# A planned order for the small work behind an expert's twelve weight blocks, in a hybrid GLA / pooling / mixture-of-experts layer

## The chip, the cores and the metric

The kernel runs on one core of one Trainium2 chip. The metric is the device time of one execution in microseconds (us); the time of a kernel is the median of its runs. The engines are PE (TensorE: matrix products and transposes), DVE (VectorE), ACT (ScalarE), POOL (GpSimd) and SP (SyncE, which here only issues DMAs).

## The reference

One layer: a mixer (gated linear attention beside multi-scale pooling), then 32 experts of which each token uses 4, then a final norm. The change touches only the expert part and the norm behind it. Cut to these:

```python
def moe(h, w_router, b_router, w_gu, b_gu, w_down, b_down):     # h: 1024 tokens x 1024
    logits = xt @ w_router + b_router                           # 32 experts
    top_vals, top_idx = lax.top_k(logits, 4)
    weights = jax.nn.softmax(top_vals, axis=-1)
    # tokens sorted by expert, each expert padded to blocks of 128
    def expert_block(xblk, e):
        gate, up = jnp.split(xblk @ w_gu[e] + b_gu[e], 2, axis=-1)     # 1024 -> 2 x 1024
        gate = jnp.minimum(gate, 7.0)
        up = jnp.clip(up, -7.0, 7.0)
        act = (up + 1.0) * gate * jax.nn.sigmoid(1.702 * gate)
        return act @ w_down[e] + b_down[e]                             # 1024 -> 1024
    # each token sums its 4 experts' rows, weighted
h = h + g2 * moe(modulate(rmsnorm(h, norm_mlp_w), sh2, sc2), ...)
return rmsnorm(h, final_norm_w)
```

All of it is float32. The kernel gets near float32 products out of TensorE by splitting each operand into a high and a low part and adding three products.

## The kernel before

The first quarter of the time is the mixer, which the change leaves alone. Then come 32 passes, one for each expert, in an order made of "heavy" experts (H, ranks 0 to 15 by number of tokens, which have more tokens than one block of 128 rows and so one or two remainder groups of 32 slots) and "light" ones (L, no remainder): HHHLLH, then LH twelve times, then LL.

**Blocks.** An expert's weights come as twelve blocks of 1 MB: eight of `w_gu` (128 rows x 2048) and four of `w_down`. SP loads them in program order into eight slots (`ring`, `mix`, `ringx`), five blocks ahead (`load_to`). Two blocks ahead, `split_to` makes the high and low parts in a tile `hl`, of which there are three: ACT copies (L131), then DVE subtracts (L132). PE then multiplies: `gu_chunk(e, k)` does 12 matmuls of 512 columns into `pG` for each of the eight k, `dn_chunk(e, k0)` 12 into `pD` for each of four k0. After k = 3 and k = 7 a heavy expert's `gu_chunk` also does its remainder products into `pR`, from the raw slots. A pass of the outer loop `e` runs the eight gate/up blocks of expert e and then the four down blocks of expert e - 1, so a block's place in the pass is 0 to 11.

**Small work between the blocks.** PE is kept in program order (`T.strict`), so what is called after a block stands in PE's queue there. DVE, ACT and POOL instructions are placed by the scheduler, unless pinned (`keep_in_program_order`). The pieces are:

- `prep_a(e-1, 0)`, `(…, 1)`: four transposes of the last expert's activation (`at`) into the one PSUM bank `pps`, an ACT copy and a DVE subtract into `aT`; `prep_a(e-1, 2)`: two transposes (`ppr`) of a remainder, an ACT copy, for a heavy e - 1 only.
- `prep_x(e+1, 0)`, `(…, 1)`, `(…, 2)`: the same for the next expert's gathered tokens (`xg` into `xT`, `xq` into `xqT`); part 2 for a heavy e + 1 only.
- `prep_sel(e+2)`, `prep_route(e+2)`: slot selection on DVE, 8 to 72 small matmuls (`pq`), gathers of expert e + 2's rows on POOL.
- `act(e)`: gate and up clipped and multiplied, three DVE instructions and one on ACT (L1533 to L1536).

`pps`, `ppr`, `pq`, and at the start `pbq`, `px`, `pyw`, `pcs`, `pblk`, all take the pool `ptr` with the tag `t`, which has one buffer: a piece's PE instruction waits until the piece before it has been read out of that bank.

The places are fixed by

```python
    A_AT, X_AT = (0, 2, 3), (4, 6, 7)
```

with `prep_sel` at 6 and `prep_route` at 9 (for e = 0 at 7). Ahead of the first pass stand, in PE's order, the four bias products `bias_rows`, `route_weights`, and the slot weights of experts 0 and 1; between the passes 0 and 1 stands `route_blocks`.

**The end.** `final_out` adds for each of eight token tiles the last expert's share (L1658, DVE), squares and sums it (ACT), takes the root (two POOL instructions of one column, L1662 and L1663), and scales by it and the norm's weight: in one DVE instruction (L1671), but for the tiles 0 and 2 on ACT (L1668) and POOL (L1669). Then the tile is stored.

Of the kernel before, what the change touches and what calls it, by code (L numbers as in the profile page):

```python
# [9 lines left out]
F32 = mybir.dt.float32  # L10
# [4 lines left out]
AF = mybir.ActivationFunctionType  # L15
ALU = mybir.AluOpType
# [3 lines left out]
P = 128  # L20
D = 1024
# [5 lines left out]
NE = 32  # L27
# [25 lines left out]
def tile_hybrid_layer(ctx: ExitStack, tc: tile.TileContext, x, c, ctx_in, c_ctx, w_ada, b_ada, norm_mix_w,  # L53
# [1173 lines left out]
    def route_weights():  # L1227
# [19 lines left out]
        for j in range(4):  # L1247
            S.activation(g2r[32 * j:32 * j + 32], g2b[32 * j:32 * j + 32, 256 * j:256 * j + 256], AF.Copy)

    def route_blocks():  # L1250

        erb = tp.tile([NE, 2 * NE + 1], F32, name="erb")
        V.tensor_copy(erb[:, 0:NE], pe_[:NE, 0:NE])
        nb = tp.tile([NE, 1], F32, name="nb")
        tmp1 = tp.tile([NE, 1], F32, name="tmp1")
        over = tp.tile([NE, 1], F32, name="over")
        pcs = ptr.tile([NE, 8], F32, name="pcs", tag="t")
        T.matmul(pcs[:, 0:1], eqr[:NE], cnt[:NE], start=True, stop=True)
        V.tensor_tensor(over, pcs[:, 0:1], cap4, op=ALU.subtract)
        for j in range(7):  # L1260
            dst = nb if j == 0 else tmp1
            V.tensor_scalar(dst, over, float(P * j), None, op0=ALU.is_gt)
            if j:
                V.tensor_tensor(nb, nb, tmp1, op=ALU.add)
        pb = ptr.tile([P, 3, NE], F32, name="pblk", tag="t")
        nbb = tp.tile([NE, 2, MAXBLK], F32, name="nbb")
        V.tensor_copy(nbb[:, 0], nb.to_broadcast([NE, MAXBLK]))
        V.tensor_copy(nbb[:, 1], capc.to_broadcast([NE, MAXBLK]))
        T.matmul(pb[:MAXBLK, 0], nbb[:, 0], linc, start=True, stop=True)
        T.matmul(pb[:MAXBLK, 1], nbb[:, 0], ident[:NE, :NE], start=True, stop=True)  # L1270
# [40 lines left out]

    bq = ap.tile([P, 4, 512], BF16, name="bq", tag="bq")

    def bias_rows():
        perm = ap.tile([P, 2 * D], BF16, name="perm", tag="y")[:, 0:1536].rearrange(
            "p (a q n j i) -> p a q n j i", a=3, q=4, n=4, j=8)
        V.memset(perm, 0.0)
        for i in range(3):
            V.tensor_copy(perm[:, i, :, :, :, i], pbd.rearrange("p n (q j) -> p q n j", q=4))
        for q in range(4):  # L1320
            pb = ptr.tile([P, 512], F32, name="pbq", tag="t")
            for i in range(3):
                T.matmul(pb, perm[:, i, q].rearrange("p n j i -> p (n j i)"), bt[:, i], start=(i == 0), stop=(i == 2))
            S.activation(bq[:, q], pb, AF.Copy)
# [108 lines left out]
    def prep_a(e, part):  # L1433
        if part == 0:
            R["aT", e] = (xp.tile([P, 2, KT, P], F32R, name="aTl", tag="xT") if e == NE - 1 else
                          ap.tile([P, 2, KT, P], F32R, name="aT", tag="aT"))
        if part < 2:
            transpose_split(R["act", e], part, R["aT", e])
        else:
            R["aqT", e] = []  # L1440
            for src in R["actq", e]:
                dst = ap.tile([P, 2, P], F32, name="aqT", tag="aqT", bufs=2)
                transpose_rem(src, dst)
                R["aqT", e].append(dst)
# [82 lines left out]
                                 rquart[:, 2 * h + j // 2, jj:jj + 1].to_broadcast([P, CAPR]),  # L1527
                                 bq[:, s_, 256 * (j % 2):256 * (j % 2) + 256], start=False, stop=False)

    def act_unit(gate, up, w, tag, bufs):  # L1530
        g = ap.tile([P, w], F32, name="ag", tag="ag" + tag)
        t = ap.tile([P, w], F32, name="at", tag="at" + tag, bufs=bufs)
        V.tensor_scalar(g, gate, 7.0, None, op0=ALU.min)  # L1533
        S.activation(g, g, AF.Gelu_apprx_sigmoid)  # L1534
        V.tensor_scalar(t, up, 1.0, -6.0, op0=ALU.add, op1=ALU.max)
        V.scalar_tensor_tensor(t, t, 8.0, g, op0=ALU.min, op1=ALU.mult)  # L1536
        return t

    def act(e):
        g, rs = GU.pop(e)  # L1540
        R["actq", e] = [act_unit(r[:, 0:256], r[:, 256:512], 256, "r", 2) for r in rs]
        R["act", e] = act_unit(g[:, 0:2].rearrange("p a n -> p (a n)"), g[:, 2:4].rearrange("p a n -> p (a n)"),
                               D, "m", 1)

    def dn_start(e):
        d = (pgu.tile([P, 4, 512], F32, name="pDl", tag="g")[:, 2:4] if e == NE - 1 else
# [148 lines left out]
    with tc.high_priority():  # L1695
# [18 lines left out]
        pinned[0] = False  # L1714
        for p_ in range(3):
            prep_x(0, p_)
    bias_rows()
    route_weights()
    dump("posm", posm)
    dump("wfull", lg)  # L1720
    for i in range(2):
        pq = ptr.tile([P, 3, 8], F32, name="pq", tag="t")
        route_main(i, pq, slice(2, 5))
        route_rem(i, pq, slice(2, 5))
        slot_weights(i, pq)
    T.strict = True
    A_AT, X_AT = (0, 2, 3), (4, 6, 7)
    for e in range(nexp + 1):
        if e < nexp:
            gu_start(e)  # L1730
            for k in range(KT):
                advance()
                gu_chunk(e, k)

                if e > 0 and k in A_AT:
                    prep_a(e - 1, A_AT.index(k))
                if e + 1 < NE and k in X_AT:
                    prep_x(e + 1, X_AT.index(k))
                if e + 2 < NE and k == 6:
                    prep_sel(e + 2)  # L1740
                if e + 2 < NE and k == 7 and e == 0:
                    prep_route(e + 2)
        if e > 0:
            dn_start(e - 1)
            for k0 in range(0, KT, 2):
                advance()
                with tc.high_priority() if e == NE - 1 else ExitStack():
                    if k0 == 0 and e < nexp:
                        act(e)
                    if e == NE - 1 and k0 >= 4:  # L1750
                        prep_a(e, k0 // 2 - 2)
                dn_chunk(e - 1, k0)
                if k0 == 2 and e + 2 < NE:
                    prep_route(e + 2)
# [158 lines left out]
```

## Time and profile before

| | |
|---|---|
| median of 3 runs | 2020.53 us (2020.08 to 2022.52) |
| profiled execution: its time, and its span | 2023.95 us, 2022.2 us |
| PE busy, share of the span | 1872.5 us, 93% |
| DVE busy | 1544.6 us, 76% |
| ACT busy | 1139.1 us, 56% |
| POOL busy | 339.0 us, 17% |
| mean of TensorE's granted clock | 0.971 of full speed |
| two passes (one H, one L) in the steady part | 88.2 us |

The profiled execution is one execution; its time is 3.4 us above the median. The span is what the profile's clock shows from the first instruction to the last, and 1.75 us lie around it. Busy shares are averages over the whole program: the expert passes, from 558 us on, have a PE that is almost never idle, and the stretch from 508 to 558 us has one that mostly is.

### The profile page before, as it was taken

To read this page: it belongs to the slowest core of one execution; us is meant where nothing else is said; L and a number is where in the kernel's file an instruction comes from. 1 tells how busy PE (TensorE), PEld (TensorE's weight loads), DVE (VectorE), ACT (ScalarE), POOL (GpSimd) and SP (SyncE) were. 2 spreads that over 40 slices of the span, in tenths; PEclk is the share of its full clock that TensorE was granted. 3 is DMA by queue.
4 is the path that set the end of the run, shared out by engine and by line. 5 is a ranking of instruction groups with operands and counts; after the bars stand their busy time and mean duration, and the time that the engine had idled before them with its cause. 6 is when DMAs were issued, how large, how long until landed. Compare 5 with 4: busy or idle time off the path is not lost.

```text
span 2022.2 us, 29473 instructions
## 1 busy us (share of the span) xinstructions
PE 1872.5 (93%) x11472; PEld 1373.6 (68%) x11473; DVE 1544.6 (76%) x1606; ACT 1139.1 (56%) x1267; POOL 339.0 (17%) x238
## 2 busy tenths in 40 slices
PE   7999998999389999999999999999999999999995
PEld 4776776787256677767677676767667676767774
DVE  5486478658667788878788788878878887887887
ACT  4564456644435566656566565656656565665664
POOL 2010043011300221111111111111111111111114
PEclk9999998999599999999999999999999999999998
DMA  9285422243635789968888796888879688887985
GB/s 343 78 295 180 152 75 92 77 151 134 237 159 199 285 327 332 357 248 355 297 317 326 283 367 246 348 305 316 324 286 366 246 343 302 322 324 290 365 305 178
DMA packets 125528, 532.33 MB, mean 263 GB/s; under 512 B 13196, under 2 KB 27328, under 8 KB 90568
## 3 DMA queue, kind: packets, MB, share of 16 engines
q1 hardware_dynamic: 109464, 481.82, 61.2%
q0 software_dynamic: 15344, 48.01, 9.1%
q8 instruction: 92, 1.51, 0.3%
q10 hardware_dynamic: 576, 0.56, 0.1%
q14 instruction: 52, 0.43, 0.1%
HBM read 497.68 MB, written 32.67 MB: 262 GB/s over the span
## 4 chain that ended last, share of the span: by engine, by line
PE 78%; DVE 9%; ACT 5%; issue 4%; DMA 3%; POOL 1%; SPq 0%; POOLq 0%; DVEq 0%; ACTq 0%
PE pG L74 31%; PE pD L74 17%; PE pa L74 12%; PE pR L74 9%; ACT hl L131 4%; DVE hl L132 3%; PE pw L74 2%; PE pps L79 2%; PE pt L74 2%; DMA ringx<-in_w_down_dram 1%; PE pt L79 1%; PE ppr L79 1%; PE pDl L74 1%; PE pq L74 1%; DVE xT L1413 1%
## 5 line engine op out<-in xcount | busy, mean ns | idle before, releaser
L74 PE MATMUL pG<-hl,xT 128*128 128x512 f32 x3072 | 769.2, 402 | 0.0
L74 PEld LDWEIGHTS pG<-hl,xT 128*128 128x128 f32 x3072 | 566.0, 189 | 144.3 <-issue 21.9
L132 DVE TENSOR_TENSOR hl<-ring,hl 128x2048 fp32r<-128x2048 f32 (+2 forms) x199 | 398.4, 2009 | 168.9 <-ACT hl L131 167.4
L131 ACT ACTIVATE hl<-ring 128x2048 fp32r<-128x2048 f32 (+2 forms) x199 | 331.9, 1670 | 304.2 <-PE pG L74 168.2
L132 DVE TENSOR_TENSOR hl<-mix,hl 128x2048 fp32r<-128x2048 f32 x144 | 329.5, 2290 | 121.8 <-ACT hl L131 121.8
L131 ACT ACTIVATE hl<-mix 128x2048 fp32r<-128x2048 f32 (+1 forms) x146 | 277.7, 1902 | 234.4 <-PE pG L74 168.7
L74 PE MATMUL pD<-hl,aT 128*128 128x512 f32 x1488 | 365.5, 401 | 0.3 <-DVE hl L132 0.3
L74 PEld LDWEIGHTS pD<-hl,aT 128*128 128x128 f32 x1488 | 276.6, 189 | 76.0 <-issue 11.7
L132 DVE TENSOR_TENSOR hl<-ringx,hl 128x2048 fp32r<-128x2048 f32 x96 | 219.7, 2288 | 24.5 <-ACT hl L131 24.2
L131 ACT ACTIVATE hl<-ringx 128x2048 fp32r<-128x2048 f32 x96 | 184.0, 1917 | 93.0 <-PE pG L74 54.5
L1374 POOL DMA_INDIRECT xg<-h2d,ix x32 | 64.4, 2012 | 884.3 <-DVE ix L1370 424.8
L74 PE MATMUL pa<-hl,hi 128*128 128x512 f32 x544 | 180.4, 417 | 5.7 <-DVE wsg L760 3.7
L1588 POOL DMA_INDIRECT acc<-y,ix x31 | 104.5, 3369 | 156.8 <-DVE y L1583 156.8
L74 PEld LDWEIGHTS pa<-hl,hi 128*128 128x128 f32 x544 | 102.5, 197 | 31.4 <-DVE wsg L760 4.8
L74 PE MATMUL pa<-hl,lo 128*128 128x512 f32 x272 | 107.7, 407 | 0.0
L74 PE MATMUL pa<-hi,hl 128*128 128x512 f32 (+1 forms) x288 | 95.6, 395 | 1.0 <-ACT hi L400 1.0
L74 PEld LDWEIGHTS pa<-hi,hl 128*128 128x128 f32 x288 | 54.9, 193 | 16.2 <-ACT hi L400 2.9
L1593 POOL DMA_INDIRECT acc<-yq,ixr x17 | 34.0, 1999 | 163.5 <-DMA acc<-y,ix 150.1
L74 PEld LDWEIGHTS pa<-hl,lo 128*128 128x128 f32 x272 | 52.8, 196 | 11.9 <-issue 1.1
L74 PE MATMUL pa<-lo,hl 128*128 128x512 f32 (+1 forms) x144 | 55.3, 387 | 1.8 <-DVE lo L401 1.8
L74 PE MATMUL pR<-ring,xqT 128*32 128x512 f32 x408 | 53.3, 596 | 0.0
L1534 ACT ACTIVATE ag<-ag 128x1024 f32<-128x1024 f32 (+1 forms) x49 | 40.7, 831 | 20.7 <-DVE ag L1533 20.7
(392 smaller groups left out, 2031.2 us busy)
## 6 DMA issues: line engine op xcount, KB each, us to landing
ring<-in_w_gu_dram SPq DMA_DIRECT2D x96, 1024.0 KB, 15.3
mix<-in_w_gu_dram SPq DMA_DIRECT2D x96, 1024.0 KB
ringx<-in_w_gu_dram SPq DMA_DIRECT2D x64, 1024.0 KB, 6.8
ring<-in_w_down_dram SPq DMA_DIRECT2D x48, 1024.0 KB
mix<-in_w_down_dram SPq DMA_DIRECT2D x48, 1024.0 KB, 18.6
ringx<-in_w_down_dram SPq DMA_DIRECT2D x32, 1024.0 KB, 16.5
ring<-in_w_in_dram SPq DMA_DIRECT2D x32, 512.0 KB, 5.4
ring<-in_w_ada_dram SPq DMA_DIRECT2D x16, 1024.0 KB, 5.8
```

The source lines that it names most:

```text
L74: i = nc.tensor.matmul(*a, **k)
L79: i = nc.tensor.transpose(*a, **k)
L131: S.activation(hl[:, 0], src, AF.Copy)
L132: i = eng.tensor_tensor(hl[:, 1], src, hl[:, 0].bitcast(F32), op=ALU.subtract)
L1374: nc.gpsimd.indirect_dma_start(out=xg, out_offset=None, in_=h2d, in_offset=bass.IndirectOffsetOnAxis(ap=ix[:, 0:1], axis=0))
L1413: V.tensor_tensor(dst[:, 1, part], pp, dst[:, 0, part].bitcast(F32), op=ALU.subtract)
L1534: S.activation(g, g, AF.Gelu_apprx_sigmoid)
L1588: nc.gpsimd.indirect_dma_start(out=acc, out_offset=bass.IndirectOffsetOnAxis(ap=ix[:, 0:1], axis=0), in_=y, in_offset=None, compute_op=ALU ...
L1593: nc.gpsimd.indirect_dma_start(out=acc4, out_offset=bass.IndirectOffsetOnAxis(ap=ixr[g][:, 0:1], axis=0), in_=yq, in_offset=None, compute_ ...
```

## The change

The places of the pieces become a table, `plan(e)`, which holds for each of the twelve places of a pass the functions to call behind that block.

- `prep_a` goes from places (0, 2, 3) to (0, 2, 4), `prep_x` from (4, 6, 7) to (5, 7, 9), `prep_sel` from 6 to 8, `prep_route` from 9 to 10.
- The four bias products, `route_weights` and the slot weights of experts 0 and 1, which stood ahead of expert 0's first block, go behind blocks of passes 0 and 1. `route_blocks` is cut in three; its counting and its row building go behind blocks 3 and 6 of pass 1. Expert 2's `prep_route` goes from place 7 of pass 0 to place 1 of pass 1.
- For the last expert `act` is called ahead of `advance()` (which issues the next load and split) and its four instructions are pinned.
- The final norm's scaling is done on DVE for all eight tiles.

```diff
-    bias_rows()
-    route_weights()
-    for i in range(2):
+    perm = bias_perm()
+
+    def weigh(i):
         pq = ptr.tile([P, 3, 8], F32, name="pq", tag="t")
         route_main(i, pq, slice(2, 5))
         route_rem(i, pq, slice(2, 5))
         slot_weights(i, pq)
...
+    def plan(e):
+        todo = {}
+
+        def at(k, f, *a):
+            todo.setdefault(k, []).append((f, a))
+        if e == 0:
+            for k, q in ((0, 0), (2, 2), (4, 1)):
+                at(k, bias_rows, perm, q)
+            at(1, route_weights)
+            at(3, prep_x, 1, 2)
+            at(5, weigh, 0)
+            at(5, weigh, 1)
+            at(6, prep_x, 1, 0)
+            at(7, prep_x, 1, 1)
+            at(7, prep_sel, 2)
+            return todo
...
+        for k, p in ((0, 0), (2, 1), (4, 2)):
+            at(k, prep_a, e - 1, p)
+        if e + 1 < NE:
+            for k, p in ((5, 0), (7, 1), (9, 2)):
+                at(k, prep_x, e + 1, p)
+        if e == 1:
+            at(1, prep_route, 2)
+            at(3, route_counts)
+            at(6, route_rows)
+            at(11, bias_rows, perm, 3)
+        if e + 2 < NE:
+            at(8, prep_sel, e + 2)
+            at(10, prep_route, e + 2)
+        return todo
...
-                if e > 0 and k in A_AT:
-                    prep_a(e - 1, A_AT.index(k))
-                if e + 1 < NE and k in X_AT:
-                    prep_x(e + 1, X_AT.index(k))
...
+                if k0 == 0 and e == NE - 1:
+                    act(e)
                 advance()
+                if k0 == 0 and e < NE - 1:
+                    act(e)
...
-        FP = dbg.get('FP', (0, 2))
+        FP = dbg.get('FP', ())
```

**What stands where.** Three places show how the instructions moved. First PE at the start of the expert passes; `pps` and `ppr` are the transposes of expert 0's tokens, `pG<-hl,xT` a gate/up block, `pbq` the bias products, `px` and `pyw` those of `route_weights`. Before:

```order
L79 MATMUL pps<-ident,xg_4733 128x128 x8
L79 MATMUL ppr<-ident,xq 128x128 x4
L74 LDWEIGHTS perm
L74 MATMUL pbq<-mix,perm 128x512
...
L79 MATMUL px<-ident,lg 128x128 x2
L74 MATMUL pyw<-pbd,wT 128x128 x2
L74 LDWEIGHTS sel
L74 MATMUL pq<-info,sel 128x3
```

And of the change:

```order
L79 MATMUL pps<-ident,xg_4733 128x128 x8
L79 MATMUL ppr<-ident,xq 128x128 x4
L74 MATMUL pG<-hl,xT 128x512 x12
...
L74 MATMUL pG<-hl,xT 128x512 x12
L79 MATMUL px<-ident,lg 128x128 x2
L74 MATMUL pyw<-pbd,wT 128x128 x2
L74 MATMUL pG<-hl,xT 128x512 x12
```

The first block of expert 0 now stands right behind its transposes, and the products for biases and weights stand between blocks.

Second, PE in a light expert's pass between two heavy ones, from the second `prep_a` transposes on. Before:

```order
L79 MATMUL pps<-ident,at 128x128 x4
L74 MATMUL pG<-hl,xT 128x512 x12
L79 MATMUL ppr<-ident,at 128x128 x2
L74 MATMUL pG<-hl,xT 128x512 x12
L79 MATMUL pps<-ident,xg_7762 128x128 x4
L74 MATMUL pG<-hl,xT 128x512 x24
L79 MATMUL pps<-ident,xg_7762 128x128 x4
L74 MATMUL pG<-hl,xT 128x512 x12
L79 MATMUL ppr<-ident,xq 128x128 x2
L74 MATMUL pD<-hl,aT 128x512 x24
```

And of the change:

```order
L79 MATMUL pps<-ident,at 128x128 x4
L74 MATMUL pG<-hl,xT 128x512 x24
L79 MATMUL ppr<-ident,at 128x128 x2
L74 MATMUL pG<-hl,xT 128x512 x12
L79 MATMUL pps<-ident,xg_7778 128x128 x4
L74 MATMUL pG<-hl,xT 128x512 x24
L79 MATMUL pps<-ident,xg_7778 128x128 x4
L74 MATMUL pD<-hl,aT 128x512 x24
L79 MATMUL ppr<-ident,xq 128x128 x2
L74 MATMUL pD<-hl,aT 128x512 x12
```

Between a `pps` and the `ppr` behind it there are now two blocks (x24) where there was one (x12); the second `pps` of the next expert's tokens stands behind the last gate/up block.

Third, DVE at the same place, from the first subtract for `xT` on (`ag`, `at` are `act`). Before:

```order
L1413 TENSOR_TENSOR xT<-pps,xT 128x512
L132 TENSOR_TENSOR hl<-mix,hl 128x2048
L132 TENSOR_TENSOR hl<-ringx_4706,hl 128x2048
L1413 TENSOR_TENSOR xT<-pps,xT 128x512
L1533 TENSOR_SCALAR ag<-pG 128x1024
L1535 TENSOR_SCALAR at<-pG 128x1024
L132 TENSOR_TENSOR hl<-ringx_4707,hl 128x2048
L1536 SCALAR_TENSOR_TENSOR at<-at,ag 128x1024
```

And of the change:

```order
L1423 TENSOR_TENSOR xT<-pps,xT 128x512
L132 TENSOR_TENSOR hl<-ringx_4706,hl 128x2048
L1543 TENSOR_SCALAR ag<-pG 128x1024
L1545 TENSOR_SCALAR at<-pG 128x1024
L132 TENSOR_TENSOR hl<-ringx_4707,hl 128x2048
L1423 TENSOR_TENSOR xT<-pps,xT 128x512
L1546 SCALAR_TENSOR_TENSOR at<-at,ag 128x1024
```

The second subtract for `xT` now stands behind the first two instructions of `act` and one more split. For the last expert, DVE's and ACT's rows from `act` to the last store of the down products are the same in both kernels, in the same order, up to the final norm.

## Rows read from the trace of the kernel before

**Rows 1.** The chain that ended last, by engine, shares of the span.
```profile
PE 78%; DVE 9%; ACT 5%; issue 4%; DMA 3%; POOL 1%; SPq 0%; POOLq 0%; DVEq 0%; ACTq 0%
```

**Rows 2.** Waits of the whole span: us in total, times, longest us.
```profile
PE ppr L79 <- DVE xT L1413: 24.0, 14, 2.1
PE ppr L79 <- DVE aT L1413: 23.8, 14, 1.7
```

**Rows 3.** Timeline, a light pass: start us, us, what, [idle before <-releaser].
```profile
1025.50 0.44 PE L79 MATMUL ppr<-ident,at 128*128 128x128 f32 x2 [1.70 <-DVE aT L1413]
...
1034.61 0.60 PE L79 MATMUL pps<-ident,xg 128*128 128x128 f32 x4
...
1039.71 0.44 PE L79 MATMUL ppr<-ident,xq 128*128 128x128 f32 x2 [1.70 <-DVE xT L1413]
1039.90 5.84 PE L74 MATMUL pD<-hl,aT 128*128 128x512 f32 x24
...
1036.76 2.29 DVE L132 TENSOR_TENSOR hl<-ringx,hl 128x2048 fp32r<-128x2048 f32 x1 [0.50 <-ACT hl L131]
1038.97 0.68 DVE L1413 TENSOR_TENSOR xT<-pps,xT 128x512 fp32r<-128x512 f32 x1
1039.57 1.22 DVE L1533 TENSOR_SCALAR ag<-pG 128x1024 f32<-128x1024 f32 x1
1040.70 1.22 DVE L1535 TENSOR_SCALAR at<-pG 128x1024 f32<-128x1024 f32 x1
...
1034.81 1.92 ACT L131 ACTIVATE hl<-ringx 128x2048 fp32r<-128x2048 f32 x1 [0.88 <-PE pG L74]
```

**Rows 4.** Stretches: us, busy of PE, PEld, DVE, ACT, POOL, PEclk, DMA, GB/s.
```profile
540.00:558.00 18.00, 8.73 (x130) 4.15 (x129) 5.23 (x7) 7.69 (x9) 0.00 (x0) 0.50 0.68 280
558.00:566.00 8.00, 8.00 (x31) 6.37 (x26) 2.69 (x4) 1.92 (x1) 0.00 (x0) 0.70 0.01 2
...
970.00:1058.00 88.00, 84.59 (x516) 61.70 (x515) 72.56 (x51) 53.07 (x37) 14.66 (x6) 1.00 0.83 314
```

**Rows 5.** Timeline of PE, passes 0 and 1 and what stands ahead.
```profile
538.55 0.69 PE L79 MATMUL ppr<-ident,xq 128*128 128x128 f32 x2 [1.39 <-ACT xqT L1419]
...
556.11 0.94 PE L74 MATMUL pq<-info,sel 128*128 128x3 bf16 x72 [5.36 <-ACT info L1246]
...
557.96 13.62 PE L74 MATMUL pG<-hl,xT 128*128 128x512 f32 x48
...
598.54 0.44 PE L79 MATMUL ppr<-ident,xq 128*128 128x128 f32 x2
...
605.02 0.31 PE L74 MATMUL pblk<-linc,nbb 32*32 32x32 f32 x2 [3.64 <-DVE nbb L1267]
...
610.66 0.60 PE L79 MATMUL pps<-ident,at 128*128 128x128 f32 x4
```

**Rows 6.** Timeline, the final norm.
```profile
1992.97 2.36 DVE L1658 TENSOR_TENSOR ring<-pF,ring 128x1024 f32<-128x1024 f32 x2 [0.90 <-PE pF L74]
...
1997.69 2.42 POOL L1669 TENSOR_TENSOR ring<-ring,fw 128x1024 f32<-128x1024 f32 x1 [0.15 <-ACT ring L1668]
...
1997.96 3.23 DVE L1671 SCALAR_TENSOR_TENSOR ring<-ring,fr,fw 128x1024 f32<-128x1024 f32 x1
...
2003.38 1.27 DVE L1671 SCALAR_TENSOR_TENSOR ring<-ring,fr,fw 128x1024 f32<-128x1024 f32 x1
...
2011.62 1.32 POOL L1662 TENSOR_SCALAR fs<-fs 128x1 f32<-128x1 f32 x1
...
2013.62 1.28 DVE L1671 SCALAR_TENSOR_TENSOR mix<-mix,fr,fw 128x1024 f32<-128x1024 f32 x1 [0.77 <-POOL fr L1663]
```

**Rows 7.** Timeline, PE in the last pass.
```profile
1968.95 1.02 PE L79 MATMUL pps<-ident,at 128*128 128x128 f32 x4 [3.84 <-DVE at L1536]
```

**Rows 8.** Transfers into `ringx`, 960 to 1062 us: ns, first and last start, landing.
```profile
L1467 SPq DMA_DIRECT2D ringx<-in_w_down_dram x2: 373/378/384, 1013.0 to 1016.4; - x2
...
DMA to landing us min/median/max: 6.5/7.4/16.4
```

More of the change, by code (lines that the diff above doesn't have):

```diff
@@ L1248, in route_weights, with route_counts @@
             S.activation(g2r[32 * j:32 * j + 32], g2b[32 * j:32 * j + 32, 256 * j:256 * j + 256], AF.Copy)
+    B = {}
     def route_blocks():
-        erb = tp.tile([NE, 2 * NE + 1], F32, name="erb")
+        erb = B["erb"] = tp.tile([NE, 2 * NE + 1], F32, name="erb")
         V.tensor_copy(erb[:, 0:NE], pe_[:NE, 0:NE])
+    def route_counts():
         nb = tp.tile([NE, 1], F32, name="nb")
@@ L1264, in route_blocks, with route_rows @@
                 V.tensor_tensor(nb, nb, tmp1, op=ALU.add)
-        pb = ptr.tile([P, 3, NE], F32, name="pblk", tag="t")
-        nbb = tp.tile([NE, 2, MAXBLK], F32, name="nbb")
+        nbb = B["nbb"] = tp.tile([NE, 2, MAXBLK], F32, name="nbb")
         V.tensor_copy(nbb[:, 0], nb.to_broadcast([NE, MAXBLK]))
         V.tensor_copy(nbb[:, 1], capc.to_broadcast([NE, MAXBLK]))
+    def route_rows():
+        nbb, erb = B["nbb"], B["erb"]
+        pb = ptr.tile([P, 3, NE], F32, name="pblk", tag="t")
         T.matmul(pb[:MAXBLK, 0], nbb[:, 0], linc, start=True, stop=True)
@@ L1312, in tile_hybrid_layer, with bias_perm @@
     bq = ap.tile([P, 4, 512], BF16, name="bq", tag="bq")
-    def bias_rows():
+    def bias_perm():
         perm = ap.tile([P, 2 * D], BF16, name="perm", tag="y")[:, 0:1536].rearrange(
@@ L1319, in bias_rows @@
             V.tensor_copy(perm[:, i, :, :, :, i], pbd.rearrange("p n (q j) -> p q n j", q=4))
[L1320 to L1324, printed above, removed]
+        return perm
+    def bias_rows(perm, q):
+        pb = ptr.tile([P, 512], F32, name="pbq", tag="t")
+        for i in range(3):
+            T.matmul(pb, perm[:, i, q].rearrange("p n j i -> p (n j i)"), bt[:, i], start=(i == 0), stop=(i == 2))
+        S.activation(bq[:, q], pb, AF.Copy)
     slots = RS + [MS[0], MS[2], MS[3]] + RX
@@ L1528, in gu_chunk, with act_unit @@
                                  bq[:, s_, 256 * (j % 2):256 * (j % 2) + 256], start=False, stop=False)
-    def act_unit(gate, up, w, tag, bufs):
+    def act_unit(gate, up, w, tag, bufs, pin=lambda i: i):
         g = ap.tile([P, w], F32, name="ag", tag="ag" + tag)
         t = ap.tile([P, w], F32, name="at", tag="at" + tag, bufs=bufs)
[L1533 to L1536, printed above, removed]
+        pin(V.tensor_scalar(g, gate, 7.0, None, op0=ALU.min))
+        pin(S.activation(g, g, AF.Gelu_apprx_sigmoid))
+        pin(V.tensor_scalar(t, up, 1.0, -6.0, op0=ALU.add, op1=ALU.max))
+        pin(V.scalar_tensor_tensor(t, t, 8.0, g, op0=ALU.min, op1=ALU.mult))
         return t
@@ L1542, in act @@
         R["act", e] = act_unit(g[:, 0:2].rearrange("p a n -> p (a n)"), g[:, 2:4].rearrange("p a n -> p (a n)"),
-                               D, "m", 1)
+                               D, "m", 1, *([tc.keep_in_program_order] if e == NE - 1 else []))
     def dn_start(e):
@@ L1716, in tile_hybrid_layer @@
             prep_x(0, p_)
-    bias_rows()
-    route_weights()
-    dump("posm", posm)
-    dump("wfull", lg)
-    for i in range(2):
+    perm = bias_perm()
+    def weigh(i):
         pq = ptr.tile([P, 3, 8], F32, name="pq", tag="t")
@@ L1725, in tile_hybrid_layer, with extras @@
         slot_weights(i, pq)
+    def plan(e):
[13 more added lines that the diff above has]
+            return todo
+        if e == NE:
+            return todo
[12 more added lines that the diff above has]
+            at(10, prep_route, e + 2)
+        return todo
     T.strict = True
-    A_AT, X_AT = (0, 2, 3), (4, 6, 7)
     for e in range(nexp + 1):
+        todo = plan(e)
+        def extras(k):
+            for f, a in todo.pop(k, ()):
+                f(*a)
         if e < nexp:
@@ L1733, in tile_hybrid_layer @@
                 gu_chunk(e, k)
-                if e > 0 and k in A_AT:
-                    prep_a(e - 1, A_AT.index(k))
-                if e + 1 < NE and k in X_AT:
-                    prep_x(e + 1, X_AT.index(k))
[L1739 to L1742, printed above, removed]
+                extras(k)
         if e > 0:
@@ L1745, in tile_hybrid_layer @@
             for k0 in range(0, KT, 2):
+                if k0 == 0 and e == NE - 1:
+                    act(e)
                 advance()
+                if k0 == 0 and e < NE - 1:
+                    act(e)
                 with tc.high_priority() if e == NE - 1 else ExitStack():
-                    if k0 == 0 and e < nexp:
-                        act(e)
                     if e == NE - 1 and k0 >= 4:
@@ L1752, in tile_hybrid_layer @@
                 dn_chunk(e - 1, k0)
-                if k0 == 2 and e + 2 < NE:
-                    prep_route(e + 2)
+                if e < nexp:
+                    extras(KT + k0 // 2)
                 if e == NE:
```

## The prediction

> **What bounds the kernel now.** I read the chain of work that ended last first: PE carries 78% of it, DVE 9% [rows 1]. So the question for each part of the profile is when PE stands still, and for what. The list of waits, for PE alone, answers it for the expert passes: a `ppr` transpose waits 14 times for a DVE subtract into `xT` and 14 times for one into `aT`, 47.8 us together [rows 2], and no other wait of PE recurs there. The timeline of a light pass shows why: `ppr` stands one block behind `pps`, both need the one bank of `ptr`, and the bank is free only when DVE has subtracted, which it does behind a split of 2.29 us. That is 1.70 us each time, twice in a light pass between heavy ones [rows 3]. The stretch table then says what else could bind: in 88 us of steady passes PE is busy 84.59 us at the full clock, DVE 72.56, ACT 53.07, and the transfers' share is 0.83 [rows 4]. PE is the bound, the rest has 12% or more to spare.
>
> Two stretches differ. [...] And between passes 0 and 1 PE waits for the block counting, 3.64 us in its longest wait [rows 5]. At the end, the norm is a chain of DVE instructions [rows 6].
>
> **The change part by part.**
>
> *The first two passes.* Expert 0's last `ppr` ends at 538.55 + 0.69 = 539.24; its first block starts at 557.96 [rows 5]. In the change it starts at 539.24: its weights and transposes are ready, since the splits ran ahead. From there I rebuild pass 0. Before it took 557.96 to 598.54 = 40.6 us, with both `xT` transposes and the slow start of the clock (mean 0.70 from 558 to 566 [rows 4]), which I keep. The moved work is what PE did from 540 to 558, 8.73 us at half clock, so 4.4 at full clock; 0.4 of it, the fourth bias, goes to pass 1: 4.0. New waits: `route_weights` sends `px` to ACT and wants it back between two blocks; on ACT a split copy of 1.92 us (as in [rows 3]) stands ahead: 2.0. The two weight steps share the bank with each other and with the transposes behind them, one DVE reduce each, partly behind a split: 1.0. Sum 47.6, so pass 0 ends at 586.8, and the first block of expert 1 (2.9 us, half of the 5.84 us of two blocks in [rows 3]) at 589.7. Before, that block ended at 610.66, where `pps` follows it [rows 5]. Gain 20.9. Pass 1 then pays: routing of expert 2, counting, the last bias, 1.7 of PE work at full clock; `pblk` one block behind `pps`, the same wait as today's 1.70 [rows 3]; and some 35 small DVE instructions, 1.0 of lateness. Together 4.4. Net 16.5 us. If the waits were nil and PE took the clock up sooner, 20; if each new step waited for a whole split on ACT and on DVE (1.92 + 2.29, twice more), 8.
>
> *The `prep_a` waits.* Two blocks now lie between `pps` and `ppr`. The bank is free 5.0 us after `pps` ends as I read the timeline (the waiting `ppr` starts 1.70 late behind one block of 2.9 and its overlap), and two blocks take 5.7 to 5.8. All 14 vanish: 23.8 us [rows 2]. The bounds are 0 and 23.8; the margin of 0.7 is on each of 14 equal passes, so I take the whole.
>
> *The `prep_x` waits.* Here something takes their place. The second `pps` now stands behind the last gate/up block, and its subtract on DVE behind `act`, as the order shows. Let 0 be that block's end. Before, the split for the second down block began on ACT 0.2 us after the block before had ended (1034.61 to 1034.81), on DVE 1.95 later, and held DVE 2.21 [rows 3]. With that block's end at -2.9, DVE is free at -2.9 + 0.2 + 1.95 + 2.21 = 1.46. Then come the two clips, 1.13 each from start to start (3.72), a split 2.21 (5.93), the subtract 0.68 (6.61), and `ppr` 0.06 later. PE does the transposes in 0.35 and two down blocks in 5.8: it is there at 6.15. So `ppr` waits about 0.6 in place of 1.70. One of the 14 belongs to expert 0's own transposes ahead of the passes and stays; 13 go from 1.70 to 0.6: 14.3 us. The bounds: 0 if the wait stays whole, 22 if it goes. The next in line, the split for the last down block, is ready on DVE at about 9.9, where PE wants it at about 10: no spare, no wait. Behind it `prep_route` stands a block later and gives that block's time back.
>
> In a heavy pass the remainder products (3.6 us) stand between, and the same walk leaves every split about 1 us early.
>
> *The last expert's `act`.* The rows on DVE and ACT are the same in the same order, so nothing is gained: the wait of 3.84 us there stays [rows 7]. 0.
>
> *The final norm.* Eight adds at 1.18 (2.36 for two) and eight scalings, each 1.27 but 1.19 from start to start: 9.4 + 9.5 us on DVE, plus the last wait for the root, 0.77, and 0.2 for a row to arrive: 20.0 from 1992.97 on. Before, the last scaling ended at 2014.90, after 21.9 [rows 6]. Gain 1.9. A scaling beside POOL's multiplication took 3.23 us where one without takes 1.27 [rows 6]; two of those go, and two scalings of 1.2 come. [...]
>
> The sum against the profile's own time: 2023.95 - 16.5 - 23.8 - 14.3 - 1.9 = 1967.5. That execution lay 3.4 us above the median of the runs, so the median should come to 1964; I say **1965 us**, with 1956 to 1974 for this case alone.
>
> **The rivals.**
>
> *Nothing takes the waits' place* (0.14). The `xT` subtract beats the two blocks and pass 0 runs without new waits: 13 x 0.6 = 7.8 and 3 us more, 1954. For it: the walk's 0.6 is the difference of two sums of ten terms. Against: the order has the subtract fifth in line.
>
> *The wait stays where it was* (0.17): the second `xT` subtract comes so late, behind ACT's copy for a split that itself waits for its block, that 1.1 us of each 13 is not saved, and passes 0 and 1 pay the 8.5 us of my lower bound: 1965 + 14.3 + 8.5 = 1988. Between it and the main case lie values to 1980. For it: DVE's rows follow each other there without idle time [rows 3]; against: ACT is busy 53.07 of 88 us [rows 4].
>
> *The root is shut out each time* (0.07). If POOL's two instructions waited for a scaling in every tile, the end would be 8 x 0.77 = 6.2 slower and not 1.9 faster [rows 6]: 1971 to 1973. [...]
>
> *Slower than before* (0.04): the weights come late. The two `ringx` blocks issued at 1013.0 and 1016.4 landed at most 16.4 us later, 1029.4 and 1032.8; ACT took up the first at 1034.81 [rows 3, 8], so about 5 us are in hand, of which the shorter passes use up to 3.4. Since ACT and DVE take their instructions in turn, a late block would hold transposes and `act` too. To eat 56 us in 13 light passes it must cost 4.3 each, so the transfers must come some 6 us later than now against the passes; 60 us of loss instead of the gain would give 2025. A transfer share of 0.83 [rows 4] speaks against it.
>
> *No change* (0.02): the same mechanism at 4.3 us a light pass, 2020.
>
> **How the numbers follow.** The main case has 0.56; with the rivals above that is 1. The range of 1952 to 1982 holds the main case, the first and third rival nearly whole and the near half of the second, about 0.82. A measurement of this kernel can tell 0.2% (4 us) from no change: faster 0.94, same 0.02, slower 0.04.
>
> **What would show it.** In the profile after: expert 0's first `pG` at about 539 and not 558; the second pass's first transpose about 21 us sooner; no `ppr` waiting for `aT`; `ppr` waiting for `xT` in about 13 light passes, 0.3 to 0.9 us each; two passes in 85.5 us and not 88.2; the last expert's 3.84 us wait unchanged; the norm 2 us shorter, with no row on POOL but the roots. I am wrong if PE waits in the light pass for an `hl`, or ACT for `ringx` or `mix` to land, or if passes 0 and 1 show PE waits of more than 8 us together.

## The result, and the profile after

The changed kernel takes 1966.06 us in the median of four runs (1965.49 to 1970.1), the kernel before 2020.34 beside it; the ratio is 0.9733, with a 95% interval of 0.9716 to 0.9750. That is faster, by 54 us, and 1 us from the forecast of 1965. The sum came so close by luck: two of its terms were wrong in opposite directions. The rest of this document takes them apart.

The profiled execution took 1970.1 us (span 1968.0), the slowest of the four. The page's busy times, then the first six lines of the list of PE's waits from expert 0's last transposes to the end (us in total, times, longest us):

```profile
PE 1865.0 (95%) x11470; PEld 1373.3 (70%) x11473; DVE 1542.4 (78%) x1608; ACT 1134.6 (58%) x1265; POOL 341.9 (17%) x236
```

```profile
PE ppr L79 <- DVE xT L1423: 7.3, 13, 0.6
PE pps L79 <- DVE at L1546: 3.8, 1, 3.8
PE pyw L74 <- ACT wT L1236: 2.1, 1, 2.1
PE ppr L79 <- ACT aqT L1429: 2.1, 1, 2.1
PE pblk L74 <- DVE xT L1423: 1.7, 1, 1.7
PE pq L74 <- DVE aT L1423: 1.7, 1, 1.7
```

Against [rows 2], the 14 waits for `aT` are gone, and 13 for `xT` are 0.56 us each where twelve of them were 1.70 and one 2.07. The forecast had said 0, and 0.6. Of the single waits, the one of 3.8 us belongs to the last pass and is as before [rows 7]; the other four are the price of passes 0 and 1, and only `pyw` and `pblk` had been foreseen.

A light pass, PE and then DVE (start us, us; the rows are of the same kind of pass as [rows 3]):

```profile
846.51 5.84 PE L74 MATMUL pD<-hl,aT 128*128 128x512 f32 x24
852.91 0.44 PE L79 MATMUL ppr<-ident,xq 128*128 128x128 f32 x2 [0.56 <-DVE xT L1423]
853.11 3.04 PE L74 MATMUL pD<-hl,aT 128*128 128x512 f32 x12
855.99 0.35 PE L74 MATMUL pq<-info,sel 128*128 128x5 bf16 x8
...
847.71 1.22 DVE L1543 TENSOR_SCALAR ag<-pG 128x1024 f32<-128x1024 f32 x1
848.85 1.21 DVE L1545 TENSOR_SCALAR at<-pG 128x1024 f32<-128x1024 f32 x1
849.98 2.28 DVE L132 TENSOR_TENSOR hl<-ringx,hl 128x2048 fp32r<-128x2048 f32 x1
852.18 0.68 DVE L1423 TENSOR_TENSOR xT<-pps,xT 128x512 fp32r<-128x512 f32 x1
```

Two clips, a split, the subtract, without idle time on DVE: the chain that the walk had added up. DVE ends the subtract 0.05 us before `ppr` starts.

Passes 0 and 1 on PE, which answer to [rows 5]:

```profile
538.44 0.69 PE L79 MATMUL ppr<-ident,xq 128*128 128x128 f32 x2 [1.08 <-ACT xqT L1429]
538.78 4.65 PE L74 MATMUL pG<-hl,xT 128*128 128x512 f32 x12
...
549.16 1.22 PE L74 MATMUL pyw<-pbd,wT 128*128 128x128 f32 x4 [2.05 <-ACT wT L1236]
550.03 4.19 PE L74 MATMUL pG<-hl,xT 128*128 128x512 f32 x12
...
590.49 0.60 PE L79 MATMUL pps<-ident,at 128*128 128x128 f32 x4
...
595.58 0.63 PE L74 MATMUL pq<-info,sel 128*128 128x5 bf16 x40 [1.70 <-DVE aT L1423]
596.14 4.61 PE L74 MATMUL pG<-hl,xT 128*128 128x512 f32 x12
...
613.50 0.44 PE L79 MATMUL ppr<-ident,at 128*128 128x128 f32 x2 [2.05 <-ACT aqT L1429]
613.70 4.59 PE L74 MATMUL pG<-hl,xT 128*128 128x512 f32 x12
...
623.23 0.24 PE L74 MATMUL pblk<-linc,nbb 32*32 32x32 f32 x2 [1.70 <-DVE xT L1423]
623.53 4.61 PE L74 MATMUL pG<-hl,xT 128*128 128x512 f32 x12
...
654.42 0.60 PE L79 MATMUL pps<-ident,at 128*128 128x128 f32 x4
```

The mark at the end of pass 1 in the kernel before:

```profile
662.85 0.60 PE L79 MATMUL pps<-ident,at 128*128 128x128 f32 x4
```

Expert 0's first block starts at 538.78 where it was 557.96 [rows 5], and expert 1's first block ends (the `pps` behind it) at 590.49 and not 610.66: 20.2 us sooner. But the same `pps` of the next pass comes at 654.42, where before it was at 662.85: only 8.4 are left. Pass 1 took 63.93 us in place of 52.19. In it stand three waits, and the block behind each takes 4.6 us where a block in the steady passes takes 3.04, as the one of 853.11 above.

The last pass and the norm, which answer to [rows 7] and [rows 6]:

```profile
1917.34 0.63 PE L79 MATMUL pps<-ident,at 128*128 128x128 f32 x4 [3.84 <-DVE at L1546]
...
1941.32 3.66 DVE L1668 TENSOR_TENSOR ring<-pF,ring 128x1024 f32<-128x1024 f32 x3 [0.90 <-PE pF L74]
1944.90 1.27 DVE L1681 SCALAR_TENSOR_TENSOR ring<-ring,fr,fw 128x1024 f32<-128x1024 f32 x1
...
1945.01 1.25 POOL L1672 TENSOR_SCALAR fs<-fs 128x1 f32<-128x1 f32 x1 [0.28 <-ACT fj L1671]
...
1947.30 1.63 POOL L1673 TENSOR_TENSOR fr<-fs,nhalf 128x1 f32<-128x1 f32 x1
...
1959.77 1.28 DVE L1681 SCALAR_TENSOR_TENSOR mix<-mix,fr,fw 128x1024 f32<-128x1024 f32 x1 [0.77 <-POOL fr L1673]
```

The ledger of the two profiles, by these marks (us gained):

| stretch | forecast | measured |
|---|---|---|
| pass 0, to the end of expert 1's first block | 20.9 | 20.2 |
| pass 1 | -4.4 | -11.7 |
| pass 2's first `pps` to pass 31's (both kinds of wait) | 38.1 | 43.2 |
| last expert's `act` (3.84 us wait) | 0 | 0 |
| norm, first add to last scaling | 1.9 | 2.2 |
| behind the last scaling | 0 | 0.3 |
| span | 56.5 | 54.2 |

### The profile page after: what moved, and what is told of

It is laid out like the page before. It is cut to its first block, busy times and chain, and to the rows that moved or that the text cites. A ratio compares the mean times of both kernels' runs of the same rounds, so it can differ in the third digit from the quotient of the medians.

```text
span 1968.0 us, 29495 instructions
## 1 busy us (share of the span) xinstructions
PE 1865.0 (95%) x11470; PEld 1373.3 (70%) x11473; DVE 1542.4 (78%) x1608; ACT 1134.6 (58%) x1265; POOL 341.9 (17%) x236
## 5 line engine op out<-in xcount | busy, mean ns | idle before, releaser
L1384 POOL DMA_INDIRECT xg<-h2d,ix x32 | 73.3, 2290 | 886.9 <-DVE wc L1405 848.6
## 6 DMA issues: line engine op xcount, KB each, us to landing
ring<-in_w_gu_dram SPq DMA_DIRECT2D x96, 1024.0 KB, 14.3
```

Source lines behind the costliest of these rows:

```text
L1384: nc.gpsimd.indirect_dma_start(out=xg, out_offset=None, in_=h2d, in_offset=bass.IndirectOffsetOnAxis(ap=ix[:, 0:1], axis=0))
```

## The experiments

In all of them everything is computed. Times are medians of 4 runs, of 5 for e5 to e8; ratios are against the kernel before in the same group of runs.

**Parts undone, one at a time (e1 to e4).**

```diff
-        for k, p in ((0, 0), (2, 1), (4, 2)):
+        for k, p in ((0, 0), (2, 1), (3, 2)):
             at(k, prep_a, e - 1, p)
```

> Changed kernel with one number put back: an expert's third aT transpose is issued behind block 3 and not behind block 4, one block behind the second one's last product, as before; everything is computed. Theory, a wait of PE costs its idle time and about 0.17 us of overlap between matmuls lost behind it: the 14 waits of a ppr for aT of 1.70 us come back and the passes grow by 14 x 1.87 = 26 us, to 1992. Rival 1, my prediction's price, idle time alone: 23.8 us, 1990. Rival 2, those waits had slack behind them and the gain of the steady passes comes from elsewhere in the new order: 0 to 5 us, 1966 to 1971.

Measured: 1992.05 us, ratio 0.9849 (0.9832 to 0.9865). From PE's waits between 700 and 1880 us, and its timeline in a light pass:

```profile
PE ppr L79 <- DVE aT L1423: 23.8, 14, 1.7
```

```profile
828.32 3.04 PE L74 MATMUL pG<-hl,xT 128*128 128x512 f32 x12
833.07 0.44 PE L79 MATMUL ppr<-ident,at 128*128 128x128 f32 x2 [1.71 <-DVE aT L1423]
```

The waits are back. From pass 2's first `pps` to pass 31's the trace takes 1259.34 us, in e4, which has these transposes in the changed place, 1232.38: 27.0 for 14 waits, 1.93 each, where the list says 1.70. The timeline shows most of the rest. A block that something follows at once gives way 2.88 us after its start (853.11 to 855.99 above), though it counts as busy for 3.04; here `ppr` stands 4.75 behind the block's start. So the wait costs 1.87, the shown idle time and 0.16 of overlap. Rival 1 is 3 us short of the trace, and rival 2 is out. By the medians e1 lies 24.4 above e4, less than 27.0, since the same edit makes pass 1 shorter (58.44 us against 60.78 in e4, see e6).

```diff
+    for q in range(4):
+        bias_rows(perm, q)
+    route_weights()
+    weigh(0)
+    weigh(1)
...
-            for k, q in ((0, 0), (2, 2), (4, 1)):
-                at(k, bias_rows, perm, q)
-            at(1, route_weights)
...
-            at(1, prep_route, 2)
-            at(3, route_counts)
-            at(6, route_rows)
-            at(11, bias_rows, perm, 3)
...
             route_blocks()
+            route_counts()
+            route_rows()
```

> Changed kernel with the start as before: biases, route weights and slot weights ahead of expert 0's first block, block counting and rows between passes 0 and 1, expert 2's routing inside pass 0; everything is computed. Theory, from the two traces' checkpoints: the changed start wins 20.2 us up to expert 1's first block and loses 11.7 again in pass 1, so undoing it costs 8.4 us: 1974.5. Rival, my prediction's sum: 16.5 us, 1982.5; then pass 1's loss would have another cause than the pieces that were moved into it.

Measured: 1981.67 us, ratio 0.9796 (0.9779 to 0.9814), which is 14.0 above e4 in the same group. Neither number fits, for two reasons. This run isn't the start as before in every part: it keeps `prep_a`'s third part behind block 4, so that in pass 1 `ppr` waits 2.05 us for `aqT`, where the kernel before waits 0.47, with a block of 4.51 us behind it. From expert 0's last `ppr` to pass 2 its trace takes 126.98 us, against 124.30 in the kernel before. And 8.4 was taken from one execution: the four traces in the table below, all with the changed start, take 110.8 to 116.5 us over this stretch, 10.5 to 16.2 less than e2.

```diff
-        FP = dbg.get('FP', ())
+        FP = dbg.get('FP', (0, 2))
```

> Changed kernel with the final norm's first multiplication of two of the tiles back on Pool; everything is computed. Theory, my term: the norm grows by 1.9 to 2.2 us, 1968.2, and a scaling on DVE beside Pool's multiplication takes about 3.2 us again. Rival, the root is shut out more often without Pool's share: the norm gets shorter by 0 to 3 us, 1963 to 1966, with the roots of 1.14 to 1.63 us gone.

Measured: 1969.38 us, ratio 0.9733 (0.9714 to 0.9753), not to be told from the changed kernel by its time. By the traces the norm, first add to the end of the last scaling, takes 21.94 us in e3, 19.62 in e4 and 19.73 in the changed kernel: 2.2 to 2.3, as the theory has it. In e3's timeline a scaling beside POOL's product is long again:

```profile
1942.94 2.42 POOL L1679 TENSOR_TENSOR ring<-ring,fw 128x1024 f32<-128x1024 f32 x1 [0.15 <-ACT ring L1678]
...
1943.07 3.37 DVE L1681 SCALAR_TENSOR_TENSOR ring<-ring,fr,fw 128x1024 f32<-128x1024 f32 x1
```

```diff
-                               D, "m", 1, *([tc.keep_in_program_order] if e == NE - 1 else []))
+                               D, "m", 1)
...
-                if k0 == 0 and e == NE - 1:
-                    act(e)
                 advance()
-                if k0 == 0 and e < NE - 1:
-                    act(e)
                 with tc.high_priority() if e == NE - 1 else ExitStack():
+                    if k0 == 0 and e < nexp:
+                        act(e)
```

> Changed kernel with the last expert's activation issued behind the splits of the next down block and with priority, as before, and not pinned; everything is computed. My prediction: 0, since the wait of 3.84 us ahead of the last pass's pps is there with and without it: 1966. Rival: ACT's written order differs in the passes in the middle (the copy into xqT stands behind one or two more copies of splits than in the changed kernel), so that the pq or ppr product that reads xqT waits some 1 to 2 us in each light pass: +13 to +26 us, 1979 to 1992.

Measured: 1967.69 us, ratio 0.9732 (0.9716 to 0.9749): no difference. The traces show why: by names and sizes ACT, DVE, POOL and SP run the same instructions in the same order in both kernels, from first to last (PE's lists differ by three records of `pbq`). The edit moved nothing, so this is the changed kernel once more. The wait of 3.84 us is there, and from pass 2's first `pps` to pass 31's it takes 1232.38 us against 1232.35. The rival, another order on ACT, was not put to the test, since there is no other order.

**Why pass 1 cost more (e5, e6).** Each line is one execution; the first column counts from the start of expert 0's last `ppr`. A slow block is one of twelve matmuls that takes over 4 us; its excess is counted over 3.05.

| kernel | last `ppr` to pass 2, us | of it pass 1 | slow blocks | their excess, us | rest, us |
|---|---|---|---|---|---|
| changed | 115.98 | 63.93 | 5 | 7.4 | 108.6 |
| e5, the same again | 116.48 | 63.92 | 5 | 7.8 | 108.7 |
| e3 | 113.62 | 60.78 | 3 | 5.2 | 108.4 |
| e4 | 110.79 | 60.78 | 2 | 2.4 | 108.4 |

These four run the same instructions in passes 0 and 1 (e4 and e5 throughout). Without the slow blocks they agree within 0.3 us; with them they lie 5.7 us apart. The stretch table shows a granted clock of 0.62 and 0.67 over slow blocks, and 1.00 behind the same wait where none is slow. The changed kernel, around the waits ahead of 596.14 and 623.53 (us, busy of PE, PEld, DVE, ACT, POOL, granted clock, DMA, GB/s), and then e4 around the same two waits:

```profile
594.00:596.00 2.00, 0.42 (x32) 0.40 (x34) 1.66 (x3) 1.83 (x1) 0.00 (x0) 1.00 0.97 406
596.00:600.00 4.00, 4.00 (x43) 3.17 (x32) 3.62 (x5) 0.00 (x0) 1.44 (x1) 0.62 0.11 45
...
621.00:623.50 2.50, 0.80 (x9) 0.34 (x7) 2.17 (x2) 1.91 (x1) 0.00 (x0) 1.00 0.00 0
623.50:628.00 4.50, 4.50 (x16) 3.31 (x12) 2.98 (x6) 0.00 (x0) 0.00 (x0) 0.62 0.00 0
```

```profile
592.00:594.00 2.00, 0.40 (x2) 0.10 (x1) 2.00 (x2) 1.56 (x1) 0.00 (x0) 1.00 1.00 414
594.00:598.00 4.00, 3.90 (x57) 3.27 (x56) 3.67 (x6) 0.59 (x2) 0.92 (x1) 1.00 0.23 96
...
617.00:619.00 2.00, 0.36 (x7) 0.32 (x7) 1.67 (x3) 1.88 (x1) 0.00 (x0) 1.00 0.00 0
619.00:623.00 4.00, 4.00 (x13) 2.85 (x12) 2.89 (x6) 0.00 (x0) 0.00 (x0) 0.67 0.00 0
```

In the stretches of 2.0 to 2.5 us that hold the wait PE is busy 0.36 to 0.80 us; behind it the granted clock, 1.00 of full speed in the steady passes [rows 4], is part of the time at 0.50, as from 597 to 600 us in the changed kernel (means of 0.62 to 0.67), or, in e4 behind the first wait, not at all (1.00).

> The changed kernel once more, unaltered, so that the three beside it have its time on the same chip and pass 1 has a second look. Theory, the blocks that take 4.4 to 4.6 us behind a short wait of PE are dips of the granted clock that fall differently in every execution: the same waits (1.70, 2.05, 1.70) stand in pass 1, with two slow blocks or fewer behind them where the first look has three, and pass 1 takes 58 to 62 us and not 63.9. Rival, the slow blocks belong to the waits themselves: three of them again, 63.9. The time is 1966 to 1969 either way.

Measured: 1967.53 us, ratio 0.9740 (0.9727 to 0.9754), and pass 1 took 63.92 us with three slow blocks (4.32, 4.58, 4.39). This expectation failed: the second execution came out like the first. That the slow blocks fall differently is shown by e3 and e4, with one each in pass 1 behind the same waits, not by e5.

```diff
-            for k, q in ((0, 0), (2, 2), (4, 1)):
-                at(k, bias_rows, perm, q)
+            at(0, bias_rows, perm, 0)
             at(1, route_weights)
+            at(2, prep_x, 1, 0)
             at(3, prep_x, 1, 2)
-            at(5, weigh, 0)
-            at(5, weigh, 1)
-            at(6, prep_x, 1, 0)
-            at(7, prep_x, 1, 1)
-            at(7, prep_sel, 2)
+            at(4, weigh, 0)
+            at(4, weigh, 1)
+            at(4, prep_sel, 2)
+            at(5, prep_x, 1, 1)
+            at(7, prep_route, 2)
...
-            at(1, prep_route, 2)
-            at(3, route_counts)
-            at(6, route_rows)
+            at(3, bias_rows, perm, 2)
+            at(3, bias_rows, perm, 1)
             at(11, bias_rows, perm, 3)
+        if e == 7:
+            at(4, route_counts)
+            at(9, route_rows)
```

> Changed kernel with passes 0 and 1 laid out anew: expert 2's routing in pass 0, nothing in pass 1 but three of the biases behind blocks 3 and 11, expert 1's first transposes early in pass 0, block counting and rows in pass 7 behind blocks 4 and 9; everything is computed. Theory, the sum failed in pass 1, where each moved piece sits one block behind a product that shares its bank and so waits 1.7 to 2.05 us with a slow block behind it: without those pass 1 takes about 53 to 54 us where the changed kernel takes 60.8 to 63.9, and the kernel gains 6 to 9 us on the changed one. Rival, the work itself and the clock cost it wherever it stands: within 2 us of the changed one.

Measured: 1963.81 us, ratio 0.9710 (0.9697 to 0.9723), 3.7 below e5 and so less than the 6 to 9 expected. Pass 1 fell to 57.88 us, not to 53: the waits of `pq` and `pblk` and their slow blocks are gone, but a bias product waits 0.69 for the bank, and the wait for `aqT` stays, with a slow block behind it:

```profile
610.14 0.69 PE L79 MATMUL ppr<-ident,at 128*128 128x128 f32 x2 [2.05 <-ACT aqT L1429]
610.48 4.38 PE L74 MATMUL pG<-hl,xT 128*128 128x512 f32 x12
```

The wait for `aqT` belongs to another part of the change: in e1, with `prep_a`'s third part behind block 3, it is 0.47 as before, and pass 1 takes 58.44 us without a slow block. Behind block 4 ACT is in a split: in the changed kernel it begins one at 611.27, just behind the `ppr` of 611.07, and copies into `aqT` only at 613.09. The block counting that went to pass 7 isn't free either: from pass 2's first `pps` to pass 31's e6 takes 1233.26 us, 0.9 more than e4.

**The rest of the `xT` wait (e7 to e12).**

```diff
-            for k, p in ((5, 0), (7, 1), (9, 2)):
+            for k, p in ((5, 0), (7, 1), (11, 2)):
                 at(k, prep_x, e + 1, p)
```

> Changed kernel with the third part of an expert's xT transposes behind block 11 where it was behind block 9, so three blocks lie between its ppr and the second pps; everything is computed. Theory, the 13 waits of 0.56 us are a subtract that comes too late for two blocks, as the walk said: they vanish, at 0.56 and about 0.2 of lost overlap each, 13 x 0.75 = 9.7 us faster than the changed kernel. Rival, the wait moves to the pq product of the routing, now one block ahead of it in the same bank, or to the first product of the next pass: 0 to 3 us.

Measured: 1968.15 us, ratio 0.9741 (0.9727 to 0.9754): nothing gained. Between 700 and 1880 us the waits for `xT` are gone from PE's list, and another has their place (two of its 15, 1.1 us together, are in the changed kernel too); the timeline shows where:

```profile
PE pD L74 <- DVE hl L132: 8.5, 15, 0.9
```

```profile
848.64 0.48 PE L74 MATMUL pD<-hl,aT 128*128 128x512 f32 x1
849.68 2.83 PE L74 MATMUL pD<-hl,aT 128*128 128x512 f32 x11 [0.55 <-DVE hl L132]
...
845.61 0.69 DVE L1423 TENSOR_TENSOR xT<-pps,xT 128x512 fp32r<-128x512 f32 x1
846.21 1.22 DVE L1546 SCALAR_TENSOR_TENSOR at<-at,ag 128x1024 f32<-128x1024 f32 x1
847.34 4.49 DVE L132 TENSOR_TENSOR hl<-ring,hl 128x2048 fp32r<-128x2048 f32 x2
```

Neither theory had this place: not the transposes' bank but DVE's queue is the bound, and the fourth down block wants its split as soon as nothing else waits. A light and a heavy pass together take 85.15 us here and 85.14 in the changed kernel.

> Both of the edits beside it, the new layout of passes 0 and 1 and the third part of xT behind block 11; everything is computed. Theory: the two add up, 16 to 19 us faster than the changed kernel, about 1949. Rival: one of them fails as its own run shows, and the sum is the other's alone.

Measured: 1962.98 us, ratio 0.9707 (0.9694 to 0.9720), as e6 alone: the rival. The next edit moves 1.2 us of DVE's work behind that split (`act_late` issues the last instruction of `act`, pinned in program order):

```diff
-        pin(V.scalar_tensor_tensor(t, t, 8.0, g, op0=ALU.min, op1=ALU.mult))
+        late.append(lambda: tc.keep_in_program_order(V.scalar_tensor_tensor(t, t, 8.0, g, op0=ALU.min, op1=ALU.mult)))
...
+        if 0 < e < NE - 1:
+            at(10, act_late)
...
```

> Changed kernel in which the last instruction of each expert's activation on DVE (the product at<-at,ag, 1.2 us) is issued behind the third down block, so that it stands on DVE behind the split for the fourth down block and not ahead of it; the third xT part stays behind block 9; everything is computed. Theory, DVE's queue between the last gate/up block and the fourth down block is what PE waits for: here the xT subtract of 0.56 us is ahead of the moved product, so that wait stays and nothing is gained, 0 to 2 us against the changed kernel. Rival, the product holds up DVE for the wait that is there: 13 x 0.75 = 9.7 us faster.

Measured: 1967.62 us, ratio 0.9741 (0.9721 to 0.9762): nothing, with the 13 waits for `xT` still there (7.5 us).

> The third part of xT behind block 11, alone, once more beside the two others on this chip; everything is computed. Theory: as in the first run of it, the waits for xT are gone and 14 to 15 waits of the fourth down block for its split, 0.55 us each, stand in their place; same time as the changed kernel within 2 us. Rival: the first run was a slow one, 5 to 9 us faster.

This is e7's kernel again. Measured: 1967.72 us, ratio 0.9737 (0.9716 to 0.9758), with the same 15 waits of 8.5 us.

> Both: the third part of xT behind block 11, and the activation's product on DVE behind the split for the fourth down block; everything is computed. Theory, DVE's queue is the bound in that stretch, and each edit alone only moves the wait: together they take it away, since the split is ready 1.13 us sooner and was 0.55 us late. 13 x 0.75 = 9.7 us faster than the changed kernel, light passes of 40.4 us and not 41.1. Rival, the wait moves on to the next instruction on DVE (the selection of the next tokens, or the next gate/up block's split): 0 to 3 us.

Measured: 1955.2 us, ratio 0.9680 (0.9659 to 0.9700), 12.5 below e10 and 12.4 below e9. The two edits that each gave nothing give this together. Its timeline in the same light pass:

```profile
849.52 3.03 PE L74 MATMUL pD<-hl,aT 128*128 128x512 f32 x12
...
847.11 2.28 DVE L132 TENSOR_TENSOR hl<-ring,hl 128x2048 fp32r<-128x2048 f32 x1
849.31 1.22 DVE L1552 SCALAR_TENSOR_TENSOR at<-at,ag 128x1024 f32<-128x1024 f32 x1
```

The split ends at 849.39, before PE wants it at 849.52, and PE has no wait between 816 and 860 us. By the traces, passes 2 to 31 take 1220.75 us against 1232.41 in e10: 11.7 for 15 waits, 0.78 each, idle time and lost overlap as in e1.

> All three edits: passes 0 and 1 laid out anew, the third part of xT behind block 11, the activation's product later on DVE; everything is computed. Theory: the new layout's 3 to 6 us and the 9.7 us add up, 1952 to 1955. Rival, the wait in the light pass moves on: as the new layout alone, 1963.

Measured: 1952.23 us, ratio 0.9666 (0.9645 to 0.9687). The gains add up, and this version beats both kernels.

## Why the prediction was right, and where its steps were not

*Passes 0 and 1* was the term that was mis-sized, in its second half: 16.5 us were forecast, 8.4 came in this execution, and 7.8 to 13.5 in the four of the table above. The rebuilt pass 0 held as a sum (20.9 against 20.2): `pyw` waited 2.05 us where 2.0 was said, the weight steps 0.32 where 1.0 was said, and a slow block behind `pyw` cost 1.1 that was not in it. Its 4.4 us of moved work at full clock, half of the 8.73 at 0.50 [rows 4], is an estimate that no run shows: the two `px` take 0.38 us in the changed kernel at a granted clock of 1.00, where before they took 0.69 at 0.50, but the `pq` of the weight steps take 1.55 (0.92 and 0.63) at 1.00 and took 1.61 (0.94 and 0.67) at 0.50. Pass 1 was said to pay 4.4 and paid 11.7 in this execution, 8.6 in e3 and e4. The missing pieces: `pq` at place 1 waits 1.70 for the bank, which was the very wait that the prediction priced for `pblk` and did not look for at the other place; `ppr` at place 4 waits 2.05 for `aqT`, 1.58 more than before; and one to three blocks behind these waits run 1.3 to 1.6 us long (mean granted clock 0.62 to 0.67 over those blocks in the changed kernel and e4). Together with `pblk`'s 1.70 and some 1.5 of moved work that is 11.2 of the 11.7 (1.70 + 1.58 + 4.7 + 1.70 + 1.5). The prediction kept the slow clock of the start as it was and did not ask whether it would be low behind the new waits. Its sign of being wrong, PE waits of more than 8 us in passes 0 and 1, was missed by little: 2.05 + 0.32 + 1.70 + 2.05 + 1.70 = 7.8.

*The `prep_a` waits*: the mechanism was right, all 14 went (e1). The price was low, 1.70 for what costs 1.93: 23.8 said, 27.0 measured. The prediction read the idle column as the cost of a wait. Its 5.0 us from the end of `pps` to the free bank count from the start of `pps`; from its end they are 4.5 (1021.00 to 1025.50), so the margin was wider than it said.

*The `prep_x` waits*: 0.6 was forecast and 0.56 measured; the terms of the walk give 6.67 - 6.15 = 0.52. These waits gave the rest of the 43.2, 16.2 us, where 14.3 was said. No run puts `prep_x` back alone, so this is read from two traces, the kernel before and e1, pass by pass. The twelve light passes 6, 8, ... 28 are 1.14 us shorter each, just what their waits shrank by: 13.7. Pass 4 alone gave 3.2, since there the kernel before waited 2.07 us and its next two blocks took 7.39 in place of 5.83, at a mean granted clock of 0.77:

```profile
777.19 0.44 PE L79 MATMUL ppr<-ident,xq 128*128 128x128 f32 x2 [2.07 <-DVE xT L1413]
777.38 7.39 PE L74 MATMUL pD<-hl,aT 128*128 128x512 f32 x24
```

The heavy passes gave 0.5 together, and the passes 3, 5 and 30 lost 1.3. The remark that the split for the last down block has no spare was right too, and decided e7.

*`act`, the norm*: 0 and 1.9 against 0 and 2.2. For `act` the 3.84 us wait, unchanged, shows it; for the norm e3's trace does, where the time itself could not tell.

So 8 us too much in the start stood against 5 too little in the waits.

*The rivals*: nothing in the waits' place (0.14) failed by 0.56 us a light pass; the whole wait (0.17) failed in the steady passes, but its other half, passes 0 and 1 paying 8.5 more than the sum, came close to what happened: they gained 8.4 and not 16.5. The root shut out in each tile did not come: three of eight roots have a long instruction, and only the last is waited for, 0.77 us as before [rows 6]. Late weights did not show: between 700 and 1880 us no wait of PE or DVE is for a transfer, and one of ACT, of 1.4 us; PE waits for an `hl` in two light passes, 0.19 and 0.88 us, where the kernel before has one such wait of 0.34.

## What to carry to other kernels

A wait that is moved away must be looked for at each new place of the same resource: a piece one block behind a `pps` in the one-buffer bank waited 1.70 us at four places (`ppr` for `aT` and for `xT`, `pq`, `pblk`), and two whose copy stood behind a split on ACT (`pyw`, `ppr` for `aqT`) waited 2.05. When a wait shrinks but does not go, add up the queue of the engine behind it to the next deadline: here two edits worth nothing alone were worth 12 us together, since DVE was late by 0.55 us for two consumers in turn. And the idle column understated what a wait of PE cost: 1.70 shown, 1.93 paid (e1). An edit of the program text isn't yet an edit of the order that runs: compare the two orders before you read anything from the time, as e4 shows.

## What the runs showed of the hardware that was not expected

A wait of PE of 1.70 to 2.05 us cost another 1.1 to 1.6 in passes 0 and 1 in some executions and not in others: blocks of 3.04 us took 4.1 to 4.6 behind it, where the granted clock was 0.62 to 0.67 on average in pass 1 (changed kernel, e4). The changed kernel and e4, with the same instructions in the same order, have three slow blocks in pass 1 and one. Over all fourteen traces a slow block stands behind the wait of 3.84 us in the last pass every time (4.0 to 5.3 us), behind the one for `wT` (2.05 to 2.32) in 10 of 12, for `aqT` (2.05) in 7 of 12, behind `pblk`'s 1.70 in pass 1 in 7 of 9, and behind the 40 waits of 1.70 in the steady passes of the kernel before and e1 never (one block 3.03 to 3.05 us, two 5.83 to 5.85). The 2.07 us wait in pass 4 of the kernel before has one behind it too (7.39 for two blocks). What sets pass 1 apart stays open.

In the norm, three one-column instructions on POOL took 1.25, 1.63 and 1.14 us; the other thirteen took 0.22 to 0.25 and 0.57. What tells them apart in this trace is the DVE instruction beside them: the three began while a scaling ran, which reads two tiles in SBUF; the others began beside an add, which reads one of its two from PSUM (`pF`), or beside none. In the kernel before, five of sixteen took 1.08 to 1.63 us, and these five alone began in a scaling. Why they take longer there was not shown. In the changed kernel the scalings behind the 1.25 and the 1.63 follow without a wait for a root, and the last waits 0.77 us behind the 1.14; in the kernel before the last two wait, 0.46 us behind the 1.63 and 0.77 behind a 1.32.
